# First tap of the delta rule's convolutions on ScalarE, and the norm row brought in through a small tile

## The chip, the cores and the metric

The kernel runs on one core of one Trainium2 chip. The core has five engines that work side by side, each through its own list of instructions in order: TensorE (PE in the profile, with PEld for its weight loads), VectorE (DVE), ScalarE (ACT), GpSimd (POOL) and SyncE (SP), which here only issues transfers. Transfers are also issued from ACT's and POOL's queues. The metric is the device time of one execution in microseconds (us), the median over runs. Before the change it is 1128.49 us, the median of 3 runs that lie between 1128.32 and 1130.63.

## The reference

One layer of a decoder is computed for a prompt of 512 tokens with 16 learned meta tokens ahead of it, and for 8 samples of 8 tokens with 2048 cached tokens each. Two parts of it bear on the change.

At its start every token's row is normalised, and the result goes through one combined input projection:

```python
def rmsnorm(x, w):
    xf = x.astype(jnp.float32)
    y = xf * lax.rsqrt(jnp.mean(xf * xf, axis=-1, keepdims=True) + RMS_EPS)
    return (y * w.astype(jnp.float32)).astype(x.dtype)
...
    xn = rmsnorm(x, p['ln_mix_pre'])
    h = xn @ p['w_in']
```

A part of `h` (query, key and value of gated DeltaNet, 4 heads of 128 channels each) goes through a causal depthwise convolution of four taps, and then through SiLU:

```python
    y = sum(xp[:, j:j + t] * w[j] for j in range(width))
...
    qkv, new_gdn_conv = causal_dwconv(gdn_qkv, gdn_conv_buf, p['gdn_conv_w'])
    qkv = jax.nn.silu(qkv)
```

The rest follows in this order: differential attention of the prompt, the delta rule in chunks and differential attention of the samples over paged caches; gates, two branch projections and an output projection; a feed-forward part with a convolution of its own, and the down projection.

## The kernel before

Activations are kept with channels on the 128 partitions and tokens along the free dimension: 512 prompt tokens, 64 sample tokens, 16 meta tokens. Products in full precision are made of three: every operand is split into a high part (`hi`, rounded to the matmul's own format) and the rest (`lo`), and `hi*hi`, `hi*lo` and `lo*hi` are summed in PSUM. A weight tile is loaded by SP as `wraw`, ACT casts it to `whi` (L331) and DVE subtracts to get `wlo` (L332).

**The start** (`embed` and `embedded`, from L440 on) has an order of its own, written out by hand for PE, ACT, DVE and POOL, and nothing moves within it. The tokens come in five tiles `x` of 128 rows (the fifth has 80) with tokens on partitions. `warm` is a tile of ones, and five products of it with itself (`WARM = 5`) go to a PSUM tile that nobody reads. The row of norm weights `ln_mix_pre`, 1024 numbers, has to be on all 128 partitions: it is loaded into partition 0 of `row`, whose other partitions are zero, and two products of `row` with `one` (ones in partition 0, zero elsewhere) spread it into the two PSUM tiles `lnb`. Then for each tile: `square` (ACT, L485) sums the squares, `root` (DVE L400, then a power on POOL, L401) gives the factor `r`, `scale` (DVE, L496) multiplies by `r` and by `lnb`, half a row at a time, `turn` (PE, L437, with the identity `consts`) transposes into PSUM, `high` (ACT, L513) and `low` (DVE, L517) split the result into `xhi` and `xlo`. In between, `whigh` (ACT, L520) and `wlow` (POOL, L523) split the first weights, and the first projections run on PE through the helper `mm` (L289).

**The delta rule's inputs** (`gdn_project`) are made head by head. For key, query and value in turn the projection is computed, and `conv_tile` makes the convolution of 616 columns: ACT and DVE copy the projection from PSUM into `pre` (L754 to L758), with the earlier rows of each sequence filled in by POOL; DVE multiplies by the first tap into `cy` (L768) and adds the other three taps one by one (L770, each reads `cy` and writes it); ACT takes the tanh (L774), and DVE makes SiLU of it in three pieces (L777). There are 12 such tiles. The projection of head 0 runs beside the last of the prompt's attention; those of heads 1, 2 and 3 run beside the chain of the head before (`gdn_chain`), while the samples' attention runs as a second stream (`rest`) beside both.

**What sets the order there.** The program is written by generators that are merged by the amount of PE work done and by the waiting times in `DELAY`; what comes out is then ordered by a scheduler, engine by engine, from its own idea of how long each instruction takes. So a changed instruction can move others that have nothing to do with it. From the conv tile on, `gdn_chain` needs in turn: decays (`dd`, `dbig_low`, `dbig_up`, L856 to L885), transposes of key, query and value with sums of squares on ACT (`gjunk`, L902, L905, L912), the root of these (`grr`, DVE L400 and POOL L401), the scaled keys `kn` (L925, L926), and from there the triangular solve.

Of the kernel before, what the change touches and what calls it, by code (L numbers as in the profile page):

```python
# [12 lines left out]
AF = mybir.ActivationFunctionType  # L13
ALU = mybir.AluOpType
# [3 lines left out]
D = 1024  # L18
# [141 lines left out]
WARM = 5  # L160
# [6 lines left out]
class Body:  # L167
# [194 lines left out]
    def part(self, x, c):  # L362
        c0, hi, lo = [e for e in x if e[0] <= c[0]][-1]
        return hi[:, :, c[0] - c0 : c[1] - c0], lo[:, :, c[0] - c0 : c[1] - c0]
# [75 lines left out]
    def embed(self, pool):  # L440
        nc, a = self.nc, self.a
        with ExitStack() as stack:
            psum = self.pool(stack, "psum_e", space=PSUM)
            lnb = [self.t(psum, [128, 512], "lnb", bufs=2) for _ in range(2)]
            warm = self.t(pool, [128, 128], "warm", bufs=1)
            row = self.t(pool, [128, D], "row", bufs=1)
            one = self.t(pool, [128, 128], "one", bufs=1)
            nc.vector.memset(warm, 1.0)
            nc.vector.memset(row, 0.0)
            nc.vector.memset(one, 0.0)  # L450
            nc.vector.memset(one[0:1], 1.0)
            nc.scalar.dma_start(self.ident, a["constants"][:, 0:128])
            nc.scalar.dma_start(row[0:1], a["ln_mix_pre"])
            return self.embedded(pool, lnb, row, one, warm)

    def embedded(self, pool, lnb, row, one, warm):
        nc, a = self.nc, self.a
        xs, raws, w = [], [], a["w_in"][0]
        for i in range(5):
# [16 lines left out]
        r, y, ps = {}, {}, {}  # L476
# [4 lines left out]
        def square(i):  # L481
            x, rows = xs[i]
            junk = self.t(pool, [128, D], "junk", bufs=1)
            r[i] = self.t(self.small, [128, 1], "ss", bufs=4), self.t(self.small, [128, 1], "r", bufs=4)
            nc.scalar.activation(junk[:rows], x[:rows], AF.Square, accum_out=r[i][0][:rows])  # L485

        def root(i):
            rows = xs[i][1]
            self.rsqrt(r[i][1][:rows], r[i][0][:rows], 1.0 / D, EPS, rows, 1)
# [46 lines left out]
        with self.tc.manual_schedule(engines=engines):  # L536
            p = self.ps("s")[:, :128]
            for _ in range(WARM):
                self.mm(p, warm, warm, start=True, stop=True)
            for g in range(2):  # L540
                self.mm(lnb[g], one, row[:, 512 * g : 512 * g + 512], start=True, stop=True)
            square(0)
            root(0)
            square(1)
# [201 lines left out]
    def conv_tile(self, ps, ch, dp, dt, tail):  # L746
        nc, pool = self.nc, self.gproj
        pre = self.t(pool, [128, 531 + 88], "pre", bufs=2)
        nc.gpsimd.memset(pre[:, 0:3], 0.0)
        sv = pre[:, 531:].rearrange("p (b j) -> p b j", b=NB)  # L750
        nc.gpsimd.tensor_copy(sv[:, :, 0:3], self.cw[:, ch, 0:24].rearrange("p (b j) -> p b j", b=NB))
        (pa, ca), (pb, cb) = ps
        o = cb[0]
        nc.scalar.copy(pre[:, 19 : 19 + ca[1]], pa)  # L754
        nc.scalar.copy(pre[:, 19 + o : 531], pb[:, : CS - o])
        nc.vector.tensor_copy(sv[:, :, 3:11], pb[:, CS - o : CM - o].rearrange("p (b t) -> p b t", b=NB))
        nc.vector.tensor_copy(pre[:, 3:17], pb[:, CM + 2 - o : NT - o])
        nc.vector.tensor_copy(pre[:, 17:19], pb[:, CM - o : CM + 2 - o])  # L758
        part = ch // 4
        nc.scalar.copy(tail[:, 3 * part : 3 * part + 3], pb[:, CS - 3 - o : CS - o])  # L760
        nc.scalar.copy(
            tail[:, 9 + 24 * part : 33 + 24 * part].rearrange("p (b j) -> p b j", b=NB),
            pb[:, CS - o : CM - o].rearrange("p (b t) -> p b t", b=NB)[:, :, TS - 3 :],
        )
        n = 531 + 88 - 3
        y_ = self.t(pool, [128, n + 3], "cy", bufs=1)
        y = y_[:, 0:n]
        nc.vector.tensor_scalar(y, pre[:, 0:n], self.cw[:, ch, 24:25], None, op0=ALU.mult)  # L768
        for j in range(1, 4):
            nc.vector.scalar_tensor_tensor(  # L770
                out=y, in0=pre[:, j : j + n], scalar=self.cw[:, ch, 24 + j : 25 + j], in1=y, op0=ALU.mult, op1=ALU.add
            )
        th = pre
        nc.scalar.activation(th[:, 0:n], y, AF.Tanh, scale=0.5)  # L774

        def silu2(dst, part):
            nc.vector.scalar_tensor_tensor(  # L777
                out=dst, in0=part(th), scalar=1.0, in1=part(y_), op0=ALU.add, op1=ALU.mult
            )

        silu2(dp, lambda u: u[:, 16:528].rearrange("p (c t) -> p c t", t=128))
        silu2(dt[:, NS:NTL], lambda u: u[:, 0:16])
        silu2(dt[:, 0:NS].rearrange("p (b t) -> p b t", b=NB), lambda u: _strided(u, 531, 11, TS))
# [1574 lines left out]
def _strided(tl, start, step, inner):  # L2358
    return tl[:, start : start + NB * step].rearrange("p (b j) -> p b j", j=step)[:, :, 0:inner]
# [39 lines left out]
```

## Time and profile before

| | before |
|---|---|
| median of 3 runs | 1128.49 us |
| profiled execution | 1128.77 us |
| its span, first to last instruction | 1127.0 us |
| PE, DVE, ACT, POOL busy | 98%, 65%, 47%, 20% of the span |
| read from HBM | 145.54 MB |
| granted TensorE clock, mean over the span | 0.998 |

The profiled execution takes 1.8 us more than its span, and 0.28 us more than the median of the runs. In the profile a line such as "L768" is a line of the kernel; "out<-in" are the program's names of what is written and read; "x12" is how many such instructions are counted together; "f32" and "fp32r" are number formats. Times of waits are idle times of an engine, put down to the instruction or transfer that came last before it went on. Matmuls overlap each other, so a PE that is busy 98% of the time need not be working at its full rate. On PE a full-precision matmul or one of the kind used for `lnb` shows as two records.

### The profile page before, as it was taken

To read this page: it belongs to the slowest core of one execution; us is meant where nothing else is said; L and a number is where in the kernel's file an instruction comes from. 1 tells how busy PE (TensorE), PEld (TensorE's weight loads), DVE (VectorE), ACT (ScalarE), POOL (GpSimd) and SP (SyncE) were. 2 spreads that over 40 slices of the span, in tenths; PEclk is the share of its full clock that TensorE was granted. 3 is DMA by queue.
4 is the path that set the end of the run, shared out by engine and by line. 5 is a ranking of instruction groups with operands and counts; after the bars stand their busy time and mean duration, and the time that the engine had idled before them with its cause. 6 is when DMAs were issued, how large, how long until landed. Compare 5 with 4: busy or idle time off the path is not lost.

```text
span 1127.0 us, 22890 instructions
## 1 busy us (share of the span) xinstructions
PE 1103.0 (98%) x8348; PEld 972.2 (86%) x8348; DVE 730.4 (65%) x1891; ACT 525.3 (47%) x1264; POOL 223.0 (20%) x336
## 2 busy tenths in 40 slices
PE   8999999999999999999999999999999999999997
PEld 6887887787787787799999987899999999988886
DVE  5456667696595467476335665499999999752315
ACT  5244544464464366353334244464555555842311
POOL 3122220120110010010000003334545454300000
PEclk9999999999999999999999999999999999999999
DMA  6376335847756866733234354323333232333213
GB/s 186 89 244 193 101 94 170 273 129 249 254 157 228 291 190 220 240 90 75 57 80 139 93 160 137 116 69 99 103 89 104 87 105 76 115 112 103 85 48 122
DMA packets 167354, 156.93 MB, mean 139 GB/s; under 512 B 12307, under 2 KB 123458, under 8 KB 167241
## 3 DMA queue, kind: packets, MB, share of 16 engines
q1 hardware_dynamic: 162833, 147.08, 42.6%
q0 software_dynamic: 3008, 5.16, 1.6%
q10 hardware_dynamic: 1400, 3.22, 0.9%
q8 instruction: 66, 1.08, 0.4%
q14 instruction: 47, 0.39, 0.1%
HBM read 145.54 MB, written 9.88 MB: 138 GB/s over the span
## 4 chain that ended last, share of the span: by engine, by line
PE 82%; DVE 7%; ACT 3%; issue 3%; DMA 3%; POOL 2%; SPq 0%; DVEq 0%; ACTq 0%; POOLq 0%
PE ps_d L289 31%; PE ps_t L289 20%; PE ps_g L289 15%; PE ps_t L437 7%; PE ps_s L289 7%; PE ps_m L289 1%; DVE wlo L332 1%; ACT KT L1536 1%; DMA wraw<-in_w_out 1%; POOL grr L401 1%; DVE lw L332 1%; DVE cy L770 0%; DVE gf L1860 0%; DMA page<-in_cache_v 0%; DVE fy L2041 0%
## 5 line engine op out<-in xcount | busy, mean ns | idle before, releaser
L289 PE MATMUL ps_d<-xhi,whi 128*128 128x256 f32 (+2 forms) x696 | 213.6, 310 | 0.1
L332 DVE TENSOR_TENSOR wlo<-wraw,whi 128x512 fp32r<-128x512 f32 x190 | 143.3, 772 | 105.3 <-ACT whi L331 103.7
L289 PE MATMUL ps_d<-xhi,wlo 128*128 128x256 f32 (+2 forms) x696 | 208.8, 303 | 1.5 <-DVE wlo L332 1.5
L289 PE MATMUL ps_d<-xlo,whi 128*128 128x256 f32 (+2 forms) x696 | 207.5, 301 | 0.0
L331 ACT CAST whi<-wraw 128x512 fp32r<-128x512 f32 x190 | 113.6, 621 | 166.6 <-PE ps_d L289 73.8
L289 PEld LDWEIGHTS ps_d<-xhi,whi 128*128 128x128 f32 x696 | 130.7, 189 | 6.0 <-issue 3.7
L289 PEld LDWEIGHTS ps_d<-xhi,wlo 128*128 128x128 f32 x696 | 130.3, 189 | 3.7 <-DVE wlo L332 2.0
L289 PEld LDWEIGHTS ps_d<-xlo,whi 128*128 128x128 f32 x696 | 131.0, 190 | 2.1 <-issue 1.8
L1536 ACT COPY KT<-ps_t 128x512 f32<-128x512 f32 x106 | 57.4, 599 | 34.7 <-PE ps_t L437 32.8
L332 DVE TENSOR_TENSOR lw<-sw,hw 128x512 fp32r<-128x512 f32 x76 | 69.7, 918 | 5.3 <-ACT hw L331 5.3
L289 PE MATMUL ps_t<-fhit,hw 128*128 128x290 f32 x228 | 68.3, 300 | 0.9 <-DVE p L2064 0.6
L437 PE MATMUL ps_t<-consts,page 128*128 128x128 f32 x512 | 68.3, 279 | 0.9 <-DMA page<-in_cache_k 0.6
L437 PEld LDWEIGHTS ps_t<-consts,page 128*128 128x128 f32 x512 | 55.6, 140 | 14.6 <-issue 7.7
L289 PE MATMUL ps_t<-fhit,lw 128*128 128x290 f32 x228 | 67.7, 297 | 0.0
L289 PE MATMUL ps_t<-flot,hw 128*128 128x290 f32 x228 | 67.6, 296 | 0.0
L331 ACT CAST hw<-sw 128x512 fp32r<-128x512 f32 x76 | 46.9, 618 | 19.6 <-PE ps_g L289 12.1
L289 PEld LDWEIGHTS ps_t<-fhit,hw 128*128 128x128 f32 x228 | 43.0, 189 | 1.5 <-DVE p L2064 0.8
L289 PEld LDWEIGHTS ps_t<-flot,hw 128*128 128x128 f32 x228 | 43.2, 190 | 0.0
L289 PEld LDWEIGHTS ps_t<-fhit,lw 128*128 128x128 f32 x228 | 43.1, 189 | 0.0
L2039 ACT ACTIVATE fy<-fpre,fw 128x592 f32<-128x592 f32 x22 | 19.5, 885 | 47.6 <-DVE fpre L1999 47.6
L2041 DVE SCALAR_TENSOR_TENSOR fy<-fpre,fw,fy 128x592 f32<-128x592 f32 x44 | 36.5, 829 | 1.0 <-ACT fy L2039 0.4
L1044 POOL DMA_DIRECT2D out_new_gdn_sample<-st x4 | 3.8, 955 | 162.7 <-DVE st L1010 134.3
(721 smaller groups left out, 2888.4 us busy)
## 6 DMA issues: line engine op xcount, KB each, us to landing
page<-in_cache_k SPq DMA_DIRECT2D x128, 256.0 KB, 4.2
page<-in_cache_v SPq DMA_DIRECT2D x128, 256.0 KB, 4.4
wraw<-in_w_in SPq DMA_DIRECT2D x86, 256.0 KB, 3.0
wraw<-in_w_ffn_in SPq DMA_DIRECT2D x50, 256.0 KB, 3.0
wraw<-in_w_down SPq DMA_DIRECT2D x44, 256.0 KB, 2.9
raw<-in_w_ffn_in SPq DMA_DIRECT2D x38, 256.0 KB, 3.0
wraw<-in_w_out SPq DMA_DIRECT2D x16, 256.0 KB, 2.9
x<-in_x_prompt SPq DMA_DIRECT2D x4, 512.0 KB, 7.0
```

Source lines behind the costliest of these rows:

```text
L289: return self.nc.tensor.matmul(out, lhsT, rhs, **kw).ins
L331: self.nc.scalar.copy(hi, raw)
L332: (eng or self.nc.vector).tensor_tensor(out=lo, in0=raw, in1=hi.bitcast(F32), op=ALU.subtract)
L401: nc.gpsimd.tensor_tensor(out=dst, in0=dst, in1=self.mhalf[:rows, :n], op=ALU.pow)
L437: self.nc.tensor.transpose(out, in_, self.ident[:k, :k])
L1044: nc.gpsimd.dma_start(o["new_gdn_sample"][0, :, h].rearrange("b k v -> k b v"), state)
L1536: copy(kt[:, :, 128 * j : 128 * j + 128], tp)
L2039: nc.scalar.activation(y, pre[:, 0:592], AF.Identity, bias=fw[:, m, 19:20], scale=fw[:, m, 16:17])
L2041: nc.vector.scalar_tensor_tensor(out=y, in0=pre[:, j : j + 592], scalar=fw[:, m, 16 + j : 17 + j], in1=y, op0=ALU.mult, op1=ALU.add)
```

## The change

Two things are changed.

In the convolution tile the first tap is no longer a multiplication on DVE but a scaled copy on ACT (the function Identity with the tap as its scale). The other three taps stay on DVE, the tanh on ACT.

At the start the norm row is loaded into a tile of its own, `line`, of one partition. This transfer is now the first that ACT issues, ahead of the identity, and waits for nothing; before, it was the second and waited until DVE had set `row` to zero. Two copies on DVE, half a row each, then bring `line` into partition 0 of `row`; they stand ahead of the first `root`. After the two products that spread the row, five more products of `warm` are issued, ahead of the first transposes.

```diff
@@ embed
             warm = self.t(pool, [128, 128], "warm", bufs=1)
+            line = self.t(pool, [1, D], "line", bufs=1)
             row = self.t(pool, [128, D], "row", bufs=1)
             one = self.t(pool, [128, 128], "one", bufs=1)
+            nc.scalar.dma_start(line, a["ln_mix_pre"])
+            nc.scalar.dma_start(self.ident, a["constants"][:, 0:128])
             nc.vector.memset(warm, 1.0)
             nc.vector.memset(row, 0.0)
             nc.vector.memset(one, 0.0)
             nc.vector.memset(one[0:1], 1.0)
-            nc.scalar.dma_start(self.ident, a["constants"][:, 0:128])
-            nc.scalar.dma_start(row[0:1], a["ln_mix_pre"])
-            return self.embedded(pool, lnb, row, one, warm)
+            return self.embedded(pool, lnb, line, row, one, warm)
@@ embedded
             for _ in range(WARM):
                 self.mm(p, warm, warm, start=True, stop=True)
             for g in range(2):
+                c = slice(512 * g, 512 * g + 512)
+                nc.vector.tensor_copy(row[0:1, c], line[:, c])
+            for g in range(2):
                 self.mm(lnb[g], one, row[:, 512 * g : 512 * g + 512], start=True, stop=True)
+            for _ in range(WARM):
+                self.mm(p, warm, warm, start=True, stop=True)
             square(0)
             root(0)
@@ conv_tile
-        nc.vector.tensor_scalar(y, pre[:, 0:n], self.cw[:, ch, 24:25], None, op0=ALU.mult)
+        nc.scalar.activation(y, pre[:, 0:n], AF.Identity, scale=self.cw[:, ch, 24:25])
```

How this stands on the engines at the start: on PE, these are the first rows before. `ps_s` is the PSUM tile of the products of ones, `ps_t` those of the transposes.

```order
L289 MATMUL ps_s_134<-warm_97 128x128 x5
L289 MATMUL lnb_95<-row_98,one_99 128x512
L289 MATMUL lnb_96<-row_98,one_99 128x512
L437 MATMUL ps_t_159<-consts_66,xs_152 128x128 x4
L437 MATMUL ps_t_169<-consts_66,xs_152 128x128 x4
```

And now:

```order
L289 MATMUL ps_s_135<-warm_97 128x128 x5
L289 MATMUL lnb_95<-row_99,one_100 128x512
L289 MATMUL lnb_96<-row_99,one_100 128x512
L289 MATMUL ps_s_135<-warm_97 128x128 x5
L437 MATMUL ps_t_167<-consts_66,xs_160 128x128 x4
```

The five products have come in between the spreading of the row and the first transposes, which cannot pass them. On DVE the start now reads:

```order
L452 MEMSET row_99 128x1024
L453 MEMSET one_100 128x128
L719 MEMSET gc_963 128x40
L454 MEMSET one_100 1x128
L543 COPY row_99<-line_98 1x512 x2
L400 TENSOR_SCALAR r_152<-ss_151 128x1
L497 SCALAR_TENSOR_TENSOR xs_160<-x_107,r_152,lnb_95 128x512
```

Only the two copies are new there; the factor `r` and the scaling follow them. After that every engine has the same order as before until the first convolution tile of head 0.

The second place is the stretch in which head 0's chain begins beside the convolution of head 1's key. On ACT it read (`er` and `dtbig` belong to the decays, `gjunk` are the sums of squares, `pre` from `ps_d` is the next tile's copy, `pre` from `cy` the tanh):

```order
L760 COPY tail_3215<-ps_d_3252 128x3
L761 COPY tail_3215<-ps_d_3252 128x24
L866 ACTIVATE er_3296<-ps_g_3297 128x80
L879 ACTIVATE er_3296<-ps_g_3306 128x512
L902 ACTIVATE gjunk_3325,gss_3321<-ps_t_3326 128x128
L754 COPY pre_3414<-ps_d_3356 128x256
L902 ACTIVATE gjunk_3325,gss_3321<-ps_t_3326 128x128 x2
L874 ACTIVATE dtbig_low_3300<-dtbig_low_3300 80x80
```

And now (line numbers are higher by 6 from here on):

```order
L766 COPY tail_3223<-ps_d_3260 128x3
L767 COPY tail_3223<-ps_d_3260 128x24
L774 ACTIVATE cy_3295<-pre_3285,cw_677 128x616
L872 ACTIVATE er_3304<-ps_g_3305 128x80
L885 ACTIVATE er_3304<-ps_g_3314 128x512
L880 ACTIVATE dtbig_low_3308<-dtbig_low_3308 80x80
L760 COPY pre_3422<-ps_d_3364 128x256
L880 ACTIVATE dtbig_up_3311<-dtbig_up_3311 80x80
L780 ACTIVATE pre_3285<-cy_3295 128x616
L891 ACTIVATE dbig_low_3320<-dbig_low_3320 128x512
```

The tap stands ahead of the decays, and the sums of squares have moved behind the tanh and the decays. On DVE in the same stretch before:

```order
L861 TENSOR_SCALAR gut_3210<-consts_66,g_657 80x80
L768 TENSOR_SCALAR cy_3287<-pre_3277,cw_669 128x616
L893 MEMSET gss_3321 128x10
L900 COPY kn_3323<-ps_t_3326 128x512
L770 SCALAR_TENSOR_TENSOR cy_3287<-pre_3277,cw_669,cy_3287 128x616
L870 SCALAR_TENSOR_TENSOR dtbig_low_3300<-ps_g_3297,gc_955,consts_66 80x80
L770 SCALAR_TENSOR_TENSOR cy_3287<-pre_3277,cw_669,cy_3287 128x616
L870 SCALAR_TENSOR_TENSOR dtbig_up_3303<-ps_g_3297,gc_955,consts_66 80x80
L770 SCALAR_TENSOR_TENSOR cy_3287<-pre_3277,cw_669,cy_3287 128x616
L881 TENSOR_TENSOR dd_3310<-ps_g_3306,gc_955 128x512
```

And now:

```order
L867 TENSOR_SCALAR gut_3218<-consts_66,g_665 80x80
L776 SCALAR_TENSOR_TENSOR cy_3295<-pre_3285,cw_677,cy_3295 128x616
L876 SCALAR_TENSOR_TENSOR dtbig_low_3308<-ps_g_3305,gc_963,consts_66 80x80
L776 SCALAR_TENSOR_TENSOR cy_3295<-pre_3285,cw_677,cy_3295 128x616
L876 SCALAR_TENSOR_TENSOR dtbig_up_3311<-ps_g_3305,gc_963,consts_66 80x80
L776 SCALAR_TENSOR_TENSOR cy_3295<-pre_3285,cw_677,cy_3295 128x616
L887 TENSOR_TENSOR dd_3318<-ps_g_3314,gc_963 128x512
```

The multiplication by the first tap is gone from DVE, and the copy of the transposed keys `kn` has moved from its place ahead of the taps to one behind the decays. From the first tile of head 0 to the start of head 3's triangular solve the order of PE, DVE, ACT and SP differs in many such places; what follows is in the same order as before.

More of the change, by code (lines that the diff above doesn't have):

```diff
@@ L451, in embed, with embedded @@
             nc.vector.memset(one[0:1], 1.0)
-            nc.scalar.dma_start(self.ident, a["constants"][:, 0:128])
-            nc.scalar.dma_start(row[0:1], a["ln_mix_pre"])
-            return self.embedded(pool, lnb, row, one, warm)
-    def embedded(self, pool, lnb, row, one, warm):
+            return self.embedded(pool, lnb, line, row, one, warm)
+    def embedded(self, pool, lnb, line, row, one, warm):
         nc, a = self.nc, self.a
```

## The prediction

> **What bounds the kernel now.** I read the busy times and the chain that ended last first.
>
> ```profile
> PE 1103.0 (98%) x8348; PEld 972.2 (86%) x8348; DVE 730.4 (65%) x1891; ACT 525.3 (47%) x1264; POOL 223.0 (20%) x336
> PE 82%; DVE 7%; ACT 3%; issue 3%; DMA 3%; POOL 2%; SPq 0%; DVEq 0%; ACTq 0%; POOLq 0%
> ```
>
> PE bounds the kernel as a whole, and the change takes no useful product from it, so it can only win what PE loses in waiting. I therefore asked for the busy time of the engines by stage (columns: stretch, its length, PE, PEld, DVE, ACT, POOL busy with instructions, clock, DMA share, GB/s): the start, the stage with the convolution tiles, and three stretches of 30 us in which a head's chain begins beside the next head's convolutions.
>
> ```profile
> 0.00:25.00 25.00, 20.11 (x121) 16.23 (x122) 14.74 (x33) 14.74 (x27) 10.87 (x23) 1.00 0.64 182
> 25.00:165.00 140.00, 137.43 (x1101) 117.20 (x1101) 81.71 (x322) 59.37 (x156) 32.13 (x62) 1.00 0.49 146
> 165.00:500.00 335.00, 325.98 (x3037) 261.76 (x3036) 220.13 (x742) 176.05 (x493) 43.36 (x71) 1.00 0.66 210
> ...
> 225.00:255.00 30.00, 28.83 (x242) 25.40 (x244) 27.20 (x75) 19.23 (x61) 7.80 (x11) 1.00 0.44 132
> 305.00:335.00 30.00, 28.34 (x227) 25.03 (x225) 26.51 (x75) 17.77 (x58) 5.74 (x7) 1.00 0.59 181
> 400.00:430.00 30.00, 28.41 (x236) 25.26 (x233) 26.00 (x70) 20.08 (x60) 4.60 (x3) 1.00 0.51 161
> ```
>
> PE is idle 4.9 us of the first 25, and 9.0 us of the 335 of the delta rule. In the three stretches it is DVE that is nearly full (27.2, 26.5 and 26.0 of 30), PE idle 1.2, 1.7 and 1.6, ACT at two thirds.
>
> The start, in order of time (start, length, engine, line, operation, and in brackets the idle time before it with what ended it):
>
> ```profile
> 0.75 0.42 ACTq L452 DMA_DIRECT2D consts<-in_constants  x1
> 1.11 2.50 PE L289 MATMUL ps_s<-warm 128*128 128x128 f32 x10 [1.11 <-DVE warm L448]
> 1.22 0.91 DVE L449 MEMSET row<- 128x1024 f32 x1 [0.16 <-issue]
> 2.17 0.50 ACTq L453 DMA_DIRECT2D row<-in_ln_mix_pre  x1
> 4.50 1.06 ACT L485 ACTIVATE junk<-x 128x1024 f32<-128x1024 f32 x1 [0.52 <-DMA x<-in_x_prompt]
> 5.92 0.57 POOL L401 TENSOR_TENSOR r<-r,mhalf 128x1 f32<-128x1 f32 x1 [3.29 <-DVE r L400]
> 6.68 3.67 PE L289 MATMUL lnb<-row,one 128*128 128x512 f32 x4 [3.07 <-DMA row<-in_ln_mix_pre]
> 7.03 0.60 ACT L520 CAST whi<-wraw 128x512 fp32r<-128x512 f32 x1
> 8.83 0.75 DVE L496 SCALAR_TENSOR_TENSOR xs<-x,r,lnb 128x512 f32<-128x512 f32 x1 [3.00 <-PE lnb L289]
> 10.19 0.60 PE L437 MATMUL ps_t<-consts,xs 128*128 128x128 f32 x4
> 10.39 2.06 DVE L496 SCALAR_TENSOR_TENSOR xs<-x,r,lnb 128x512 f32<-128x512 f32 x3 [0.74 <-PE lnb L289]
> 10.83 0.59 ACT L513 CAST xhi<-ps_t 128x512 fp32r<-128x512 f32 x1 [3.19 <-PE ps_t L437]
> ```
>
> The norm row's transfer waits for `row` to be zeroed, is issued at 2.17 and ends PE's idle time at 6.68. PE then spends 3.67 us on four pieces, and DVE's first scaling, whose factor was ready at 6.5, waits until 8.83. So the row, and not the tokens or their sums, sets the start. The pieces are slow: 0.92 us each, and the pieces of the ones 0.25 (2.50 over 10), where four transposes just after take 0.60, that is 0.11 apart. PE got fast 3.5 us after it had begun to work without a break at 6.68.
>
> **The change, part by part.** *The row.* The transfer is issued at 0.75, where the identity's was. How long it takes is not shown, since before it queued behind others; the nearest rows are its own time (6.55 at most as seen, 4.4 us after 2.17) and a small load on idle queues later:
>
> ```profile
> 2.17 4.38 DMA row<-in_ln_mix_pre
> 21.98 0.37 SPq L619 DMA_DIRECT2D baw<-in_w_in  x1
> 24.77 0.24 POOL L626 COPY baz<-baw 128x64 f32<-128x64 f32 x1 [1.91 <-DMA baw<-in_w_in]
> ```
>
> So it lands between 3.5 (2.8 us after the issue) and 5.1. I take 3.5, because at 0.75 hardly anything is queued ahead of it. The two copies have no row; a DVE operation on 616 columns takes 0.53 (L768, below), so 512 take about 0.45, and half a row is in place at 4.0, the other at 4.4. Behind the waiting copies on DVE stands the first `root`, and behind that POOL's power and the scaling; the sum it needs is ready at 5.7 (the square begins at 4.50, 1.06 long), so they lose nothing unless the row lands after 4.8. The identity's issue slips by 0.4; even at 4.4 us it lands by 5.6, ahead of any transpose.
>
> PE spreads the row from 4.0 instead of 6.68. If the fast rate comes 3.5 us after that, at 7.5, three pieces and a half are slow, the rest ends at about 7.6, and the five new products (ten pieces at 0.11, and the last one's tail) end at 8.8: the first transpose starts 1.4 us earlier than at 10.19. If the work from 1.11 on counts, the rate is fast from 4.6; the pieces end at 6.0 (0.4 us each), the new ones at 7.2; then the factor `r` (5.92 + 0.57) and one scaling of 0.75 set the transpose to 7.35, a gain of 2.8. I take the middle, 2.1, since only a gap of about 0.4 us lies between the ones (end 3.6) and the row. Behind it ACT's `high` comes at 8.7 instead of 10.83 and hands the 2.1 us on: the weights it splits in between are there at 7.03 already, and DVE, no longer kept by the second `lnb`, is 2.8 us ahead. After that the order is unchanged up to the first convolution, and in 25 to 165 PE works 137.4 of 140 us, waiting only for what this core itself made or asked for; so the 2.1 us pass to the end whole. The new products cost nothing else: PE would wait at that place for the scaling.
>
> The Trainium skill, in "TensorE: Matmul & The Clock Gate", Part 1, says that the PE clock is halved until about 3.4 us of sustained work, judged in windows that run freely, whatever the program does. The trace agrees with its 3.5 us. By the page the fast rate could come anywhere from 4.5 to 7.9 us, which would make the gain 1.2 to 2.8.
>
> *The tap.* The durations, from the tile `cy` and from the same operation in the feed-forward part:
>
> ```profile
> L770 DVE SCALAR_TENSOR_TENSOR cy<-pre,cw,cy x36: 837/852/861, 172.8 to 425.6; 128x616 f32<-128x616 f32 x36
> L768 DVE TENSOR_SCALAR cy<-pre,cw x12: 522/532/540, 172.2 to 423.1; 128x616 f32<-128x616 f32 x12
> L774 ACT ACTIVATE pre<-cy x12: 708/720/722, 175.5 to 426.5; 128x616 f32<-128x616 f32 x12
> L2039 ACT ACTIVATE fy<-fpre,fw 128x592 f32<-128x592 f32 x22 | 19.5, 885 | 47.6 <-DVE fpre L1999 47.6
> ```
>
> DVE loses 12 x 0.53 = 6.4 us. ACT gains 12 times 0.72 (a tanh of the same size) to 0.92 (885 ns for 592 columns, scaled to 616); I take 0.92, the same function with its scale read per partition, 11.0 us. One tile's own path gets 0.39 us longer, and by a handover from DVE's copies to ACT and one back.
>
> Head 0's three tiles lie at 172 to 205, where DVE has room. The other nine lie in the three stretches. The chain that ended last runs there through DVE, ACT and POOL, not PE (start, length, what):
>
> ```profile
> 228.65 0.45 DVE cy L768
> 230.49 0.36 ACT gjunk L902 x2
> 235.16 0.37 ACT gjunk L905 x2
> 237.59 0.45 DVE cy L768
> 238.27 3.13 POOL grr L401
> 242.54 0.85 DVE cy L770
> 246.36 0.45 DVE cy L768
> ```
>
> Three first taps of 0.45 stand in it, 1.35 us per stretch and 4.0 in all. But this is only the chain of the delta rule; PE meanwhile works for the samples' attention, and its waits in 165 to 500 are short:
>
> ```profile
> PE ps_d L289 <- DVE wlo L332: 1.5, 1, 1.5
> PE ps_t L437 <- DVE on L1049: 1.1, 2, 0.6
> PE ps_t L437 <- DVE kn L926: 1.0, 1, 1.0
> ```
>
> What PE can win is bounded by its idle time in the three stretches, 4.5 us; what it can lose, by nine taps each 0.39 us longer on the projection's path, 3.5 us, if the order were kept. It is not: from the first tile on it is another order, with the sums of squares later on ACT and fewer DVE rows between the chain's steps. That can go either way by a us or two. I take a gain of 0.5: DVE, which is short of time there, is relieved, ACT is not full (19.2 of 30 and 2.8 more), and PE's fill is the reason why most of the 4.0 us is not seen. No transfer is added, and SP's list is changed only in which of a few weight and page loads goes first.
>
> *Sum.* 2.1 + 0.5 = 2.6 us off the profiled execution's 1128.77 gives 1126.2, a span of 1124.4. The profiled execution lies 0.28 us above the median of 1128.49; against that the forecast is 1125.9.
>
> **The rivals.** *DVE was the pace of the three stretches.* For it: DVE at 27.2 of 30 and three taps in the chain. Against: PE idle only 1.2 to 1.7 us in each. Then most of the 4.0 us comes through, and with the start the time is 1128.5 - 2.1 - 3.5 = 1122.9.
>
> *ACT becomes the pace there* (the other side). In 228 to 238 ACT's sums of squares are in the chain already; the tap goes ahead of them in ACT's order, in which each waits for DVE's copies of `pre`. If nine taps of 0.92 us, 8.3 us, stood in the chain with half of it reaching PE, the loss is 4.1 against the 2.1 of the start: 1130.5, and slower once more than half reaches PE. A worse new order would look the same: PE waiting on `kn` or on `gjunk` for more than the 2.1 us that L926 and L1049 cost now. Against it: ACT has 10 us free in each stretch.
>
> *The new products stand in the way.* If PE is still slow at their start, they take 2.5 us as at 1.11 to 3.61: with the row spread at 4.0 to 7.7, the transpose starts at 10.2 and the start gains nothing; with the row landing at 5.1, it starts at 11.8, 1.6 us later than before. The time is 1128.0 to 1129.6. The page on the clock gate would have this where the gap at 3.6 spoils a window and the next full one ends past 10. Against it: PE was fast after 3.5 us of work in this trace.
>
> **How the numbers follow.** Two runs of this kernel differ by up to 0.2% (1128.32 to 1130.63), so a change within 0.2%, 2.26 us, is hard to tell from none: faster is below 1126.2, slower above 1130.7. The forecast (start -1.4 to -2.8, delta rule -1.5 to +0.5) has 0.48, from 1124.2 to 1127.6, and of it 0.28 falls below 1126.2. The first rival has 0.18, all faster. The second has 0.24, half of it slower, half the same. The third has 0.10, nearly all the same. This makes faster 0.47, same 0.39, slower 0.14. The range of 1122.5 to 1130.0 leaves out the ends of the first and the second rival. The forecast's own range is 1124.2 to 1127.6.
>
> **What would show it.** In the profile after: PE's idle time ahead of `lnb` under 0.7 us instead of 3.07; the first transpose at 7.3 to 8.8; the first convolution tile about 2 us earlier than 172.2; the tap on ACT at 0.72 to 0.92 us; DVE's busy time lower by some 5.5 us (6.4 less the copies), ACT's higher by 9 to 11; in 165 to 500 PE's idle time within a few us of 9.0. I am wrong if the stage from the first convolution to the triangular solve of head 3 changes its length by more than the 2.1 us of the start, or if the start's gain is used up by a transfer that comes no earlier.

## The result, and the profile after

The kernel became slower: 1137.33 us, the median of six runs (1135.25 to 1141.97), against 1128.60 us for six runs of the kernel before (1128.32 to 1130.63). The ratio is 1.0079, with a 95% interval of 1.0068 to 1.0091. The profiled execution takes 1137.44 us, its span is 1135.7 us, 8.7 us more than before. In the experiments below one slow run, of 2683.86 us, is among the six of the kernel with the old start and the tap on ACT: it is in its median of 1138.72 us (1138.33 without it) and not in its ratio.

The busy times of the engines, from the page of the kernel after:

```profile
PE 1108.3 (98%) x8358; PEld 977.0 (86%) x8358; DVE 728.7 (64%) x1881; ACT 530.9 (47%) x1276; POOL 224.3 (20%) x336
```

ACT is busy only 5.6 us more than before and DVE 1.7 us less, and PE stays at 98%. Busy time counts instructions that overlap once, so it moves by less than the 12 taps take by themselves (9.9 us on ACT, 6.4 on DVE). No engine became a new bound. By stage (columns as in the prediction: stretch, its length, PE, PEld, DVE, ACT, POOL busy, clock, DMA share, GB/s):

```profile
0.00:25.00 25.00, 23.33 (x152) 20.50 (x153) 16.94 (x43) 16.04 (x31) 10.85 (x23) 1.00 0.72 208
25.00:165.00 140.00, 138.07 (x1112) 118.07 (x1111) 82.44 (x325) 59.57 (x157) 32.84 (x64) 0.99 0.48 145
165.00:500.00 335.00, 320.69 (x2954) 254.65 (x2953) 211.28 (x708) 178.13 (x497) 38.57 (x66) 0.99 0.65 206
...
225.00:255.00 30.00, 28.37 (x237) 24.43 (x236) 26.43 (x73) 19.06 (x56) 5.83 (x8) 1.00 0.44 128
```

The start is better: PE is idle 1.7 of the first 25 us, before 4.9. The stage of the delta rule is worse: 14.3 of 335 us idle, before 9.0. The start in order of time (start, length, engine, line, operation, idle time before it):

```profile
0.76 0.52 ACTq L449 DMA_DIRECT2D line<-in_ln_mix_pre  x1
...
2.61 0.75 DVE L543 COPY row<-line 1x512 f32<-1x512 f32 x2
...
3.41 3.03 PE L289 MATMUL lnb<-row,one 128*128 128x512 f32 x4
...
6.16 0.75 DVE L497 SCALAR_TENSOR_TENSOR xs<-x,r,lnb 128x512 f32<-128x512 f32 x1 [0.68 <-POOL r L401]
6.27 1.28 PE L289 MATMUL ps_s<-warm 128*128 128x128 f32 x10
...
7.39 1.90 PE L437 MATMUL ps_t<-consts,xs 128*128 128x128 f32 x12
```

DVE copies the row from 2.61 us on, PE spreads it from 3.41 instead of 6.68, and the first transpose starts at 7.39 instead of 10.19. The tap and its neighbours (duration of one, min/median/max in ns, then the first and last start):

```profile
L776 DVE SCALAR_TENSOR_TENSOR cy<-pre,cw,cy x36: 841/857/862, 170.0 to 426.7; 128x616 f32<-128x616 f32 x36
...
L774 ACT ACTIVATE cy<-pre,cw x12: 800/822/842, 169.1 to 424.0; 128x616 f32<-128x616 f32 x12
```

The first tap starts at 169.1 us, 3.1 earlier than before (172.2). So the loss lies behind it. Two marks show where. The products of the branch projections read their weights `whi` and `wlo`; the first of them reads the tile `kt`, the last the tile `cy`, and both stand at the same place in the order of PE in every kernel here. Before (name, count, duration, first to last start):

```profile
L289 PE MATMUL ps_d<-kt,whi x16: 280/308/414, 607.5 to 632.0; 128*128 128x256 f32 x8, 128*128 128x322 f32 x8
L289 PE MATMUL ps_d<-cy,wlo x16: 277/297/315, 608.4 to 633.2; 128*128 128x256 f32 x8, 128*128 128x322 f32 x8
```

After:

```profile
L289 PE MATMUL ps_d<-kt,whi x16: 280/307/414, 614.1 to 641.2; 128*128 128x256 f32 x8, 128*128 128x322 f32 x8
L289 PE MATMUL ps_d<-cy,wlo x16: 280/296/315, 615.1 to 642.4; 128*128 128x256 f32 x8, 128*128 128x322 f32 x8
```

This cuts the span in four pieces, which I use for every kernel below: up to the first tap, from there to the first branch product, the branch products, and the rest. All numbers are of the profiled executions, in us.

| kernel | to first tap | tap to branch | branch | rest | span |
|---|---|---|---|---|---|
| before | 172.2 | 435.3 | 25.7 | 493.8 | 1127.0 |
| after | 169.1 | 445.0 | 28.3 | 493.3 | 1135.7 |
| difference | -3.1 | +9.7 | +2.6 | -0.5 | +8.7 |

Two losses were not foreseen: 9.7 us in the stage of the delta rule (with the gates behind it), and 2.6 us in the branch products, where neither the code nor the order of any engine was changed. What PE waits for between 165 and 500 us (us in total, times, longest):

```profile
PE ps_t L437 <- DVE kn L931: 3.4, 2, 1.8
PE ps_g L289 <- ACT gv L1034: 2.0, 2, 1.6
PE ps_t L437 <- DVE on L1055: 1.7, 2, 1.0
```

Before, where line numbers are lower by 6, the row of this `kn` and the only one of a `gv` read:

```profile
PE ps_t L437 <- DVE kn L925: 0.7, 1, 0.7
PE ps_g L289 <- ACT gv L980: 0.5, 2, 0.3
```

`kn` had 1.0 more at its other line (L926), `on` had 1.1, and the `gv` that now costs 2.0 (L1034) is not among the ten longest waits. These are steps of the delta rule's chain, not of the convolution.

### The profile page after: what moved, and what is told of

Read it like the earlier page. It is cut to its first block, busy times and chain, and to the rows that moved or that the text cites. A ratio compares the mean times of both kernels' runs of the same rounds, so it can differ in the third digit from the quotient of the medians.

```text
span 1135.7 us, 22921 instructions
## 1 busy us (share of the span) xinstructions
PE 1108.3 (98%) x8358; PEld 977.0 (86%) x8358; DVE 728.7 (64%) x1881; ACT 530.9 (47%) x1276; POOL 224.3 (20%) x336
## 4 chain that ended last, share of the span: by engine, by line
PE 83%; DVE 5%; DMA 3%; issue 3%; ACT 3%; POOL 2%; SPq 1%; DVEq 0%; ACTq 0%; POOLq 0%
PE ps_d L289 30%; PE ps_t L289 21%; PE ps_g L289 16%; PE ps_t L437 7%; PE ps_s L289 7%; DMA wraw<-in_w_out 1%; PE ps_m L289 1%; POOL grr L401 1%; ACT KT L1542 1%; DMA x<-in_x_prompt 1%; DMA wraw<-in_w_in 0%; DVE cy L776 0%; DVE wlo L332 0%; DMA page<-in_cache_v 0%; DMA page<-in_cache_k 0%
## 5 line engine op out<-in xcount | busy, mean ns | idle before, releaser
L289 PE MATMUL ps_d<-xlo,whi 128*128 128x256 f32 (+2 forms) x696 | 209.9, 305 | 0.0
L331 ACT CAST whi<-wraw 128x512 fp32r<-128x512 f32 x190 | 114.1, 620 | 168.7 <-PE ps_d L289 72.1
L289 PE MATMUL ps_s<-KT,qb 128*32 128x256 f32 x512 | 36.1, 385 | 0.4
```

The source lines that it names most:

```text
L289: return self.nc.tensor.matmul(out, lhsT, rhs, **kw).ins
L331: self.nc.scalar.copy(hi, raw)
```

## Experiments

**The tap, the order and the start, taken apart.** Three things change at once: the start, the engine that computes the tap, and the order that the scheduler makes of it. Since the generators emit the same sequence in both kernels, the order can be held: for each engine a table gives the order of the instructions from the first convolution to the triangular solve of head 3, and each instruction gets an edge (order only, no wait) to the one ahead of it. The rivals are: the order loses; the tap's longer path through ACT loses; the start loses, by the clock or by transfers moved. Each ratio below is to runs of the kernel before that were taken beside it (medians 1128.76, 1129.23 and 1129.65 us in the three rounds), so it is the ratios that can be compared between rounds.

The first kernel has the new start alone; its order in the delta rule is then the old one by itself.

```diff
@@ conv_tile, against the changed kernel
-        nc.scalar.activation(y, pre[:, 0:n], AF.Identity, scale=self.cw[:, ch, 24:25])
+        nc.vector.tensor_scalar(y, pre[:, 0:n], self.cw[:, ch, 24:25], None, op0=ALU.mult)
```

> The changed start alone; the first tap stays on DVE, and every engine keeps the old order in the delta rule. Order theory and tap theory alike: the start's 3.2 us come through whole, 1125.3 us (1124.5 to 1126.5), shift of -2.7 to -3.2 us at 600 us. Start theory (the loss of the whole change comes with the start, as half-rate windows of the TensorE clock or moved transfers): 1131 to 1137 us.

Measured: 1127.16 us, ratio 0.9982 (0.9971 to 0.9992). This is 0.7 us above the range that the order theory and the tap theory share; the branch products, 2.0 us longer than before, account for it (below).

The second has both edits and the old order, the third the new start and the new order but the tap on DVE.

```diff
@@ against the changed kernel; the third kernel also has the tap on DVE and the other table
+ORDER = {
+    "PE":
...
+}
+def pin(tc, bb):
+    every = bb.bb.instructions
...
+                i = every[n - int(first) + k]
+                if last is not None:
+                    tc.add_manual_dep(i, last.name, how, reason="pin")
+                last = i
```

> Both edits, but each engine's instructions pinned to the order of the kernel before, with the tap on ACT behind its own tile's copies. Order theory (the loss of 8.7 us comes from the order that the scheduler made of it): 1125 to 1127 us, within 1.5 us of the start alone. Tap theory (the tap's longer path through ACT is what costs): 1134 to 1138 us, close to the changed kernel.

Measured: 1129.67 us, ratio 1.0005 (0.9997 to 1.0014).

> The changed start and the new order on every engine, but the tap is computed on DVE again, just ahead of its tile's second tap. Order theory: 1135 to 1139 us, as slow as the changed kernel or slower. Tap theory: 1125 to 1128 us.

Measured: 1138.19 us, ratio 1.0080 (1.0065 to 1.0096).

The fourth is the kernel before with the tap's line alone.

```diff
@@ conv_tile, against the kernel before
-        nc.vector.tensor_scalar(y, pre[:, 0:n], self.cw[:, ch, 24:25], None, op0=ALU.mult)
+        nc.scalar.activation(y, pre[:, 0:n], AF.Identity, scale=self.cw[:, ch, 24:25])
```

> The tap on ACT with the order that comes with it, and the old start. Order theory and tap theory alike: the changed kernel less the start's gain, 1139 to 1142 us. Start theory: 1127 to 1130 us.

Measured: 1138.72 us, ratio 1.0075 (1.0062 to 1.0088); this lies 0.3 us below the range of the order theory and the tap theory.

| kernel | to first tap | tap to branch | branch | rest | span |
|---|---|---|---|---|---|
| new start alone | 168.9 | 435.3 | 27.7 | 493.5 | 1125.4 |
| both edits, old order | 168.7 | 438.4 | 27.7 | 493.3 | 1128.1 |
| new start, new order, tap on DVE | 169.3 | 446.5 | 27.7 | 493.1 | 1136.6 |
| old start, tap on ACT | 171.9 | 445.2 | 26.2 | 494.0 | 1137.3 |

The order decides. With the old order the tap on ACT costs 3.1 us in the second piece (438.4 against 435.3; by the ratios, 2.6 us); with the tap left on DVE, the new order alone costs 11.2 (446.5; by the ratios, 11.1). With the tap on ACT it costs 6.6 (445.0 of the changed kernel against 438.4), so the two do not simply add up: in the new order the move to ACT loses nothing (445.0 against 446.5 in the profiles; the ratios, 1.0079 and 1.0080, are equal). So the order theory and the tap theory both have a part, the order by far the larger, and the start theory falls: the old start with the tap on ACT is as slow as the whole change. The second kernel missed the range of the order theory (1125 to 1127 us) by 2.7 us, and that is the tap's own price. Could the edges that hold the order cost the time instead? No kernel has the edges alone, but in two kernels below they hold the old order for a while with the tap on DVE: the first tap of head 3 stands 230.0 us behind that of head 0 in one (230.5 with the new start alone, without edges), the last tap of head 1 75.0 us in the other (74.1). So they cost about a us at most.

PE's waits from 165 to 510 us, with the tap on DVE and the new order:

```profile
PE ps_t L437 <- DVE kn L931: 3.5, 2, 1.8
PE ps_t L437 <- DVE on L1055: 1.7, 2, 1.0
PE ps_g L289 <- ACT gv L1034: 1.6, 2, 1.2
```

They are those of the changed kernel, though ACT computes no tap. With both edits and the old order, the waits look otherwise:

```profile
PE ps_d L289 <- DVE wlo L332: 1.6, 1, 1.6
PE ps_t L437 <- ACT KT L1542: 1.5, 3, 0.8
...
PE ps_t L437 <- DVE kn L932: 1.2, 1, 1.2
```

Here ACT's copies `KT` for the samples' attention come late: at four of the twelve taps they stand in ACT's list just behind the tap or one instruction later. PE waits 2.3 us for `KT` in all (1.5 here and 0.8 at another product), 0.4 with the new start alone; the 1.9 us between them are the larger part of the 3.1.

**The order, in three sections.** The table of the third kernel is mixed: the new order in one section, the old in the two others, each joined where both orders have done the same instructions on an engine (at 301 to 312 us and at 411 to 432 us). The tap is on DVE, the start is new.

```diff
@@ against the kernel with the new order and the tap on DVE: each engine's list in ORDER
-    new, first section; new, second section; new, third section
+    new, first section; old, second section; old, third section
```

> Changed start, tap on DVE; the new order only in the first section (first convolution of head 0 to about 310 us, head 0's chain), the old order after it. Theory of separate losses (each section loses what the trace of the whole new order lost there and nothing is given back): 4.5 us over the start alone, 1131.7 us (1130.5 to 1133). Theory of slack (PE's lost time in a section is made up by fill later): within 1.5 us of the start alone, 1126 to 1128.7 us.

Measured: 1131.54 us, ratio 1.0017 (1.0008 to 1.0026).

> The same, with the new order only in the middle section, about 310 to 430 us (chains of heads 1 and 2). Separate losses: the trace of the whole new order went from +4.5 to about +5 us there, a half-rate window of the clock among it, so 0 to 1.5 us over the start alone, 1127 to 1128.7 us. Slack: 1126 to 1128.7 us too; this run tells instead whether some section of the new order is harmless or better than the old one.

Measured: 1133.24 us, ratio 1.0035 (1.0022 to 1.0048).

> The same, with the new order only in the last section, from about 430 us to the triangular solve of head 3. Separate losses: the trace of the whole new order went from +5 to +11.5 us there, so 5.5 to 7 us over the start alone, 1132.7 to 1134.2 us. Slack, or a loss that builds up over all sections: under 3 us over the start alone, below 1130.2 us.

Measured: 1132.35 us, ratio 1.0038 (1.0024 to 1.0051).

The first lies in the range of the theory of separate losses, the last 0.35 us below it (second piece 440.3 and 440.7 against 435.3), and both lie outside that of slack: nothing is given back later. The middle one, which I took for harmless, missed its range by 4.5 us (second piece 444.1 in its profile, the slowest of its five runs, with two half-rate windows of the clock in it). Against the new start alone (0.9982) the ratios are 0.35%, 0.53% and 0.56% higher, about 4, 6 and 6 us. Together this is 16 us where the whole new order costs 11, so the sections do not simply add up. A joint may have a price of its own, which was not measured apart: right behind the first joint, in the kernel with the new middle section, PE works 1.98 of 5 us and waits 2.4 us for `ob`.

```profile
305.00:310.00 5.00, 1.98 (x15) 1.62 (x14) 2.72 (x9) 1.68 (x4) 0.00 (x0) 0.97 1.05 388
```

How such a loss comes about is seen at the end of head 2's chain, where the chain's steps are the same in both kernels. The new start alone, with the old order (start, length, engine, line, operation, idle time before it):

```profile
460.65 0.28 PE L289 MATMUL ps_d<-xlo,whi 128*128 128x256 f32 x1
460.77 0.29 PE L289 MATMUL ps_d<-xhi,wlo 128*128 128x256 f32 x1
460.89 0.27 PE L289 MATMUL ps_d<-xhi,whi 128*128 128x256 f32 x1
...
461.12 0.26 ACT L986 COPY gv<-ps_g 80x128 f32<-80x128 f32 x1
...
461.43 0.48 PE L289 MATMUL ps_g<-gv,kn 16*128 16x128 f32 x2 [0.26 <-ACT gv L986]
```

The new order in the last section:

```profile
459.98 0.38 PE L289 MATMUL ps_g<-grhs,xyt 80*80 80x128 f32 x2
...
460.91 0.26 ACT L986 COPY gv<-ps_g 80x128 f32<-80x128 f32 x1
...
461.23 0.48 PE L289 MATMUL ps_g<-gv,kn 16*128 16x128 f32 x2 [0.86 <-ACT gv L986]
...
463.74 0.35 DVE L1024 SCALAR_TENSOR_TENSOR grhs<-ps_g,neg_eg,vn 128x128 f32<-128x128 f32 x1
...
464.15 0.49 PE L289 MATMUL ps_g<-grhs,xy 128*128 128x128 f32 x2 [0.84 <-DVE grhs L1024]
```

ACT's copy takes 0.26 us in both. In the old order the projections of the gates (`ps_d`) lie on PE between one step of the chain and the next; in the new order they have been put elsewhere, and PE stands still through the same handovers, 0.86 and 0.84 us. The chain is not slower there; its gaps are not filled. This is one place, read closely; that the other losses come about in the same way is argued from it and from the waits above.

**Is it the tap's order, or any other order?** Two kernels on top of the best one (below). One writes the tap as two instructions of half the width, still on DVE. The other changes one waiting time of the merge and no instruction.

```diff
@@ conv_tile
-        nc.vector.tensor_scalar(y, pre[:, 0:n], self.cw[:, ch, 24:25], None, op0=ALU.mult)
+        m = n // 2
+        nc.vector.tensor_scalar(y[:, 0:m], pre[:, 0:m], self.cw[:, ch, 24:25], None, op0=ALU.mult)
+        nc.vector.tensor_scalar(y[:, m:n], pre[:, m:n], self.cw[:, ch, 24:25], None, op0=ALU.mult)
```

> The best kernel so far (changed start without the second ones, tap on DVE), with the tap written as two instructions of half the width; the order that comes with this differs from the old one in many places from the first convolution on, though nothing moves to another engine. Theory that nearly any other order loses (the waiting times are fitted to the old order): 1128 to 1134 us. Theory that only moving the tap to ACT makes a bad order: 1125.5 to 1127 us, the 12 further fixed costs on DVE being hidden.

Measured: 1128.70 us, ratio 0.9992 (0.9983 to 1.0000); second piece 439.0.

```diff
@@ DELAY, first number of each head
-    16.02, 16.02, 16.02, 21.53
+    13.02, 13.02, 13.02, 18.53
```

> The best kernel so far with one waiting time (the one ahead of the convolutions' tails) 3 units less for every head; no instruction is changed, only the order. Theory that nearly any other order loses: 1128 to 1134 us. Theory that only moving the tap makes a bad order: 1124.5 to 1127 us.

Measured: 1137.78 us, ratio 1.0065 (1.0052 to 1.0078); second piece 447.2.

Without moving anything to another engine, one kernel loses 3.9 us in the second piece and the other 12.1, against 435.1 of the best kernel. Of the 3.9 a part is the tap itself, whose two halves take 0.75 us together instead of 0.53; of the 12.1 a part, 5.1 us at most, is the clock, which stood at half rate for 10.2 us of that piece. The other waiting time changes no instruction, so an order alone, with the tap on DVE, can lose 7 us and more. Two samples do not show that every order is worse, but the old one is better than the three others that were seen.

**The branch products.** They take 27.7 or 28.3 us with the new start and 25.7 or 26.2 with the old, though the program is the same there. Around 570 to 600 us the loads of the new start alone and of the kernel before are issued 3.21 us apart, to 0.01 us, up to one load of `w_out`, which takes 4.23 us instead of 2.94 (issue, time to landing, transfer; before, then the new start alone):

```profile
602.92 2.94 DMA wraw<-in_w_out
```

```profile
599.71 4.23 DMA wraw<-in_w_out
```

The next kernel tests why.

```diff
@@ embedded, against the new start alone
-            for _ in range(WARM):
-                self.mm(p, warm, warm, start=True, stop=True)
             square(0)
```

> The changed start alone as before, but without the second five products of ones; old order, tap on DVE. Theory that the ten instructions more on TensorE moved a code fetch onto a load of the output projection (a 16 KB fetch 1.0 us earlier in that stretch, the load 4.2 us instead of 2.9): that load takes 2.9 us again, the 1.9 us lost at 609 to 632 us are not lost, and with a start within 0.5 us of the other the time is 1125.0 to 1126.0 us. Theory that the stretch is paced by its loads and an earlier arrival only waits there: the loss stays, 1127 us, or 1128 us and more if the second ones were worth a us of start.

Measured: 1125.68 us, ratio 0.9970 (0.9958 to 0.9982), the fastest of all. Pieces: 169.4, 435.1, 25.8, 493.7.

Traffic during that load, in 40 slices, and the queue of the code below it (packets, MB, share of 16 engines), with the second ones:

```profile
GB/s 308 255 352 333 328 284 154 140 87 34 275 111 43 125 202 241 304 337 308 284 159 68 19 10 10 10 10 10 10 10 14 19 19 19 19 0 0 0 5 72
...
q8 instruction: 1, 0.02, 2.0%
```

Without them:

```profile
GB/s 231 304 344 311 291 344 337 350 298 198 205 165 119 60 106 185 198 205 264 297 258 271 297 311 245 212 198 330 93 53 26 26 20 20 7 0 0 0 0 0
...
q8 instruction: 1, 0.02, 2.1%
```

In both a block of code, 16 KB in one packet, is fetched during the load. With the second ones it comes 1.2 us after the load was issued and keeps one of the 16 DMA engines for 1.36 us (2.0% of 16 x 4.25 us); the last packets trickle in at 10 to 19 GB/s for over a microsecond. Without them the fetch comes 2.1 us after the issue, when the load is mostly done, and the load takes 3.0 us. Each of these traces has 66 such blocks over its span, and only PE's list differs between the two kernels: so I take it that PE's code is fetched block by block as PE gets through it, and that five more products at 6 us bring forward a fetch at 600 us. That fetch and trickle use the same DMA engine is my reading; the trace does not name the engine of a packet. The Trainium skill, in "Runtime: NRT & Kernel Launch", section "Instruction fetch mechanics", gives blocks of 16 KiB and calls the cost mostly hidden; the size agrees, but here the cost was 1.9 us (27.7 against 25.8).

The same without a new start: the kernel before with ten products of ones at its start instead of five.

```diff
-WARM = 5
+WARM = 10
```

> The kernel before with one number changed: ten products of ones instead of five at the start, into an idle time of 3.07 us of TensorE, so that the start itself should lose nothing (the five more take 1.25 us at most). Code-fetch theory: the fetch comes about 1 us earlier in the output projection's loads again, one load takes 4 us and more instead of 2.9, and 1.5 to 2.5 us are lost at 605 to 632 us: 1130.2 to 1131.2 us. Theory that the loss there came with the earlier arrival of the new start: as the kernel before, 1128.2 to 1129.2 us.

Measured: 1129.01 us, ratio 0.9997 (0.9988 to 1.0006). By the time alone this is the other theory, but the profile shows both of its parts:

```profile
1.11 4.35 PE L289 MATMUL ps_s<-warm 128*128 128x128 f32 x20 [1.11 <-DVE warm L448]
...
6.51 1.96 PE L289 MATMUL lnb<-row,one 128*128 128x512 f32 x4 [1.06 <-DMA row<-in_ln_mix_pre]
...
8.52 2.13 PE L437 MATMUL ps_t<-consts,xs 128*128 128x128 f32 x12
```

```profile
601.20 4.27 DMA wraw<-in_w_out
```

The load takes 4.27 us, its code fetch comes 1.1 us after the issue, and the branch products take 27.3 us (25.7 before): a loss of 1.6 us as the code-fetch theory has it. But the start won as much, which I had excluded: with PE busy from 1.11 to 5.46 the granted clock is full from 5.02 on instead of 10.14, the four pieces that spread the row take 1.96 instead of 3.67 us, the first transpose comes at 8.52 instead of 10.19, and the first tap 2.1 us earlier. In the measured time the two cancel.

The whole change without the second ones:

```diff
@@ embedded, against the changed kernel
-            for _ in range(WARM):
-                self.mm(p, warm, warm, start=True, stop=True)
             square(0)
```

> The changed kernel without the second five products of ones. Code-fetch theory: the 2.5 us lost at 605 to 622 us come down to 0.5 or less and the rest stays, 1135.0 to 1136.0 us. Theory that the new order alone sets that loss: 1137 to 1138 us.

Measured: 1135.32 us, ratio 1.0047 (1.0030 to 1.0064). The load takes 2.77 us instead of 4.62, the branch products 26.1 instead of 28.3, and the second piece stays as it was, at 445.6 (445.0). The branch loss therefore comes with the second ones, and not with the order. All 14 profiles agree. In the eight kernels with five more products of ones the fetch comes 0.9 to 1.2 us after the issue of that load, the load takes 4.2 to 4.8 us and the branch products 26.9 to 28.3; in the six others it comes 2.1 to 2.5 us after, the load takes 2.8 to 3.1 and the branch products 25.7 to 26.2.

## Why the prediction was wrong

*The start, -2.1 (bounds -1.4 to -2.8).* The mechanism was right, the size too small: -2.8 at the first transpose and -3.1 at the first tap; where the last 0.3 came from I did not follow. The term that was mis-sized is the landing of the row. I took 3.5 us, 2.8 after the issue, from the load of `baw`, and called that a small load on idle queues; in the trace before, it is 32 KB in 1024 packets of 32 bytes, the row one packet of 4 KB. In the profile after, that packet moved from 1.68 to 2.28 us, so the row was there 1.5 us after its issue, outside my bounds of 3.5 to 5.1. The fast rate came between my two cases of 4.6 and 7.5: the granted clock is full from 5.71 on. The transposes were then set by the factor `r` (5.56 + 0.57 on POOL) and one scaling, as in my second case. The ones at 6.27 held them back a little: 7.39 with them, 7.04 without. How far that moment moves is seen in the eleven kernels with the new start: PE has the same products up to there, and the clock is full from moments between 4.57 and 7.12 us.

*"The new products cost nothing else."* This step failed. They cost 0.35 us at that place, which vanishes by the first tap, and 1.9 to 2.2 us at 600 us, where a code fetch comes earlier. Nothing in my reading looked at the code queue. For the same reason "the 2.1 us pass to the end whole" failed: of 3.3 us won by the new start alone up to the first tap, 1.6 us are left in its span.

*The tap, -0.5 (its range -1.5 to +0.5, its outer bounds -4.5 to +3.5).* The duration was right: 0.82 us on ACT, inside 0.72 to 0.92. The upper bound seems right under its own condition: "nine taps each 0.39 us longer on the projection's path, 3.5 us, if the order were kept" stands against 3.1 measured with the order kept. That is in part luck: with the tap's measured 0.82 us the same working gives nine times 0.29, 2.6 us, and most of the 3.1 came by another path, the `KT` copies behind the tap. The value within the bounds was wrong; I let DVE's relief win, and in the old order it does not. The signs I gave for it, DVE's busy time lower by 5.5 us and ACT's higher by 9 to 11, did not come either (1.7 and 5.6).

*"It is not: from the first tile on it is another order ... That can go either way by a us or two."* This is the step by which the forecast failed. The order alone costs 11.2 us with the tap on DVE and 6.6 with it on ACT; order and tap together cost 9.7. I had compared the orders at the start of head 0's chain only and judged them by the later sums of squares. Where it was read closely, what matters is where PE's filling work stands against the handovers of the chains, and the old order does well in that: two other disturbances cost 3.9 and 12.1 us. A bound of "a us or two" had no row behind it. A better one would have been the idle time that PE could have there without fill: in the new order a handover such as `gv` or `grhs` leaves PE 0.8 us, and each of the four chains has a row of them. My own sign of being wrong came true: the stage changed its length by 9.7 us.

*The rivals.* DVE as the pace of the stretches fell: with both edits and the old order DVE is busy 4.1 us less in the second piece than with the new start alone (262.13 against 266.24), and the piece is 3.1 us longer. The second rival named the right side and partly the right place ("a worse new order would look the same: PE waiting on `kn` ..."): `kn` and `on` went from 2.8 us to 5.1. Its first half, ACT as the pace, fell as the cause of the loss: ACT is busy 178 of 335 us, and the new order is no faster without the tap on ACT; in the old order, though, the `KT` copies do hold PE up behind the tap. Its price of 4.1 us was less than half of what came. The third rival fell at its place, since the ones took 1.28 us and not 2.5; they stood in the way 590 us later.

*The chances.* Added up by their own terms they give 0.46 for faster, some 0.42 for the same and 0.12 for slower, and not 0.47, 0.39 and 0.14; the forecast does not hang on this.

What is left open: the waits with a name explain only a part of the 9.7 us. PE's idle time in the second piece rose from 9.0 to 14.3 us, the other 4.4 us are longer busy time. The same number of matmuls is in it. One half-rate window of the clock (below) lies in it, 3.41 us long and so worth 1.7 us at most; that the rest is matmuls which overlap less when they stand alone between two waits is my guess, not shown.

```profile
172.20:607.50 435.30, 426.28 (x3807) 359.61 (x3806) 267.06 (x865) 209.23 (x574) 44.43 (x69) 1.00 0.58 179
```

```profile
169.10:614.10 445.00, 430.69 (x3809) 361.96 (x3808) 263.48 (x852) 214.84 (x587) 43.39 (x69) 1.00 0.57 175
```

The first row is the second piece of the kernel before, the other that of the kernel after.

## What to carry to other kernels

Where a scheduler orders a PE-bound kernel, price an edit by the order that it makes: compare what fills PE between the steps of the dependent chains along the whole stage, and hold the order fixed to see the edit's own cost, here 3.1 us beside the 11.2 of the order. An instruction added for free at an idle place is not free if it shifts later code: look at the code queue beside transfers that the engines wait for. And take the time of a transfer from one with packets of the same size and number.

## What the hardware showed beyond this

*A half-rate clock while PE is busy.* Apart from its start and its end, the profile of the kernel after has a granted clock below 1 in two places; this is the first (kernel after, then the kernel before at the same work):

```profile
45.00:50.00 5.00, 5.00 (x33) 4.96 (x33) 1.30 (x6) 1.93 (x4) 3.01 (x3) 0.67 0.00 0
```

```profile
48.00:53.00 5.00, 5.00 (x46) 4.96 (x45) 1.30 (x6) 1.94 (x4) 2.80 (x3) 1.00 0.01 3
```

PE is busy all of the 5 us in both, but does 33 matmuls instead of 46. The trace gives a window of 3.41 us at half rate, with another at 323 us; in the 3.41 us ahead of the second, PE is busy for 1.64. The six runs of this kernel go with their mean granted clock: 1135.25 us at 0.998, 1141.97 at 0.989. The kernel before took 1128.77 us at 0.998, so at the same clock 6.5 of the 8.7 us are left; and two runs with the old start and the tap on ACT took 1136.60 and 1137.16 us at 0.999. The clock is a part of the loss, not the whole of it. The Trainium skill, in "TensorE: Matmul & The Clock Gate", Part 1, has the clock halved after an idle window of about 3.4 us; the length agrees, but in the 3.41 us ahead of the first window here the profile shows no idle time of PE. Ahead of it come products with a narrow operand (`baz` with 32 columns, then `bat` with 8 and `gcw` with 28), which may count as little work; no run tested that. When the window falls there is in the record: of the eleven kernels with the new start, the four whose clock became full between 5.58 and 6.06 us have it, 40.96 us after that moment (12 times 3.413), and the seven with 4.57 to 5.41 or 6.95 and 7.12 do not.

*Ones ahead of the row.* In the kernel with the old start, five more products of ones in the idle time before the row halved the time of the pieces that spread it (0.49 us each instead of 0.92).
